# An expert stage that gathers for four experts at once, in one-pass products

## The chip, the cores and the metric

The kernel runs on one core of a Trainium2 chip. The metric is the device time of one execution in microseconds (us), the median of several runs. A core has a matrix engine (TensorE, PE in the profile; its weight loads stand apart as PEld), a vector engine (VectorE, DVE), a scalar engine (ScalarE, ACT), GpSimd (POOL), and SyncE (SP), which here issues all large transfers. Transfers are carried out by 16 DMA engines. TensorE writes its results into PSUM, from where DVE or ACT copy them out to SBUF, the working memory.

## What is computed

Two transformer blocks on 256 tokens of width 1024, in float32. The change touches only the last part of the second block, a mixture of experts:

```python
def hier_moe(h, w_group, b_group, w_expert, b_expert, w_gate, w_up, w_down):
    t = h.reshape(-1, d); hf = t.astype(F32)
    ...                                   # router: one of 4 groups, then the two best of its 8 experts
    combine = jnp.sum(jax.nn.one_hot(global_i, N_EXPERTS, dtype=F32) * top_w[..., None], axis=1)
    out = jnp.zeros(hf.shape, F32)
    for e in range(N_EXPERTS):            # 32 experts, w_gate and w_up 1024 x 512, w_down 512 x 1024
        hid = jax.nn.silu(t @ w_gate[e]) * (t @ w_up[e])
        out = out + combine[:, e:e + 1] * (hid @ w_down[e]).astype(F32)
    return out.reshape(bsz, seq, d).astype(h.dtype)
```

Each token takes part in two experts only; for all others its `combine` is zero.

## The kernel before

The kernel is written against a tile framework: the code allocates named tiles from pools, and a scheduler of the framework puts the instructions of every engine into a fixed order when the kernel is built, by priorities and its own idea of durations. Block 1 and the rest of block 2 come first; the change does not touch their code. At their end stands the stage of the experts (`moe`, L1323), in these steps:

- **Router.** For each half of the tokens (t = 0, 1) the normed row is made in two steps: L1352 multiplies x by the norm's weights on DVE, L1373 multiplies by the reciprocal root on ACT. The two tiles `hh` stay for the whole stage. A chain of some fifty small DVE instructions (L1371 to L1417) finds the two experts of each token, their weights (`comb`), and `rank`, the place of a token in its expert's list. Each expert takes up to 64 tokens (`CAP`); a token count above 64 would run a second path behind `tc.If` (L1534 on), and every engine reads the flag `oi` for it, SP among them (TENSOR_LOAD in the order of its instructions).
- **Loop over 16 pairs of experts** (L1514). For a pair p, `prepare` (L1430) builds a one-hot matrix `oh` on DVE from `rank`, and the same times the router's weight, `ow`. TensorE multiplies the token rows by `oh`, which gathers the 2 x 64 tokens as the columns of `xg`: 8 slices of the width (k) times two halves of the tokens. `hk` (L1428) picks a slice as every 8th element of a row of `hh`. `ow` is transposed to `owT`. `hidden` (L1467) makes the gate and up products (PSUM tiles `proj`) and the gated units (tile `th`). `down` (L1481) transposes these to `hT`, multiplies by the down weights (PSUM tiles `sc`) and copies the result out into `yo`. `scatter` (L1499) multiplies by `owT`, which weights the rows and puts them back to their tokens (PSUM tiles `pv` and `tp`), and adds to x.
- The code of the loop is hidden(p), scatter(p-1), prepare(p+1), down(p).

**Products and passes.** All products go through `mm` (L145). One on float32 operands stands as two MATMUL records in the trace, one on float32r operands as one; a transpose is one. Gate, up and down keep 64 columns of weights for each of two experts in two halves of the array, and their records run side by side in twos. Gather and put-back use all 128 columns.

**Weights.** The weights of the experts are read once, in 384 loads of 512 KB: for a pair 16 for gate and up (i = 0 to 3, two experts each) and 8 for down. `fetch` (L1454) takes a buffer for each from a ring of 36 (`RING`, L42: names w, h, l, x, u, T, t, which are the buffers wraw, whi, wlo, wx, u, Thi, Tlo of the earlier blocks). A load waits on SP until its buffer is free, and every load behind it on SP waits too. The u buffers are 16 and serve rows, gathered tokens and results as well.

Of the kernel before, what the change touches and what calls it, by code (L numbers as in the profile page):

```python
# [25 lines left out]
F32 = mybir.dt.float32  # L26
F32R = mybir.dt.float32r
AF = mybir.ActivationFunctionType
OP = mybir.AluOpType
# [9 lines left out]
HPR = 600  # L39

CAP = 64
RING = "w" * 5 + "h" * 5 + "l" * 4 + "x" * 5 + "u" * 9 + "T" * 4 + "t" * 4  # L42

SH1, SH2 = 0, 4
NEG = -1e30
# [74 lines left out]
def tile_model(ctx: ExitStack, tc: tile.TileContext, I: dict, out: bass.AP):  # L120
    nc = tc.nc
    V, S, G, T = nc.vector, nc.scalar, nc.gpsimd, nc.tensor
# [3 lines left out]
    psum = ctx.enter_context(tc.tile_pool(name="psum", bufs=1, space=PS))  # L126
# [8 lines left out]
    def wtile(shape, dt, name, bufs=2):  # L135
        return (scope[0] if name in common else scope[-1]).tile(shape, dt, name=name, bufs=bufs)
# [22 lines left out]
    ident_r = const.tile([128, 128], F32R, name="ident_r")  # L159
# [1144 lines left out]
    def runit(claim=False):  # L1304
        return unit(claim, F32R)
# [17 lines left out]
    def moe(router, wb, ring):  # L1323
# [20 lines left out]
        with tc.high_priority(HPR):  # L1344

            for c in range(2):
                for t in range(2):
                    cs = slice(512 * c, 512 * c + 512)
                    tsplit(x[:, t, cs], t, pair[c])
                    sq = wtile([128, 512], F32, name="th")  # L1350
                    S.activation(sq, x[:, t, cs], AF.Square, accum_out=ss[:, t, c:c + 1])
                    V.tensor_mul(hh[t][:, cs], x[:, t, cs], wb[:, cs])  # L1352
            ps = psum.tile([128, 512], F32, name="proj", bufs=3)
            for K in range(8):
                xh, xl = pair[K // 4]
# [9 lines left out]
            rs = rstd_of(r1, 2, 1024)  # L1365
            tp = psum.tile([128, 4, 128], F32, name="tp", bufs=2)
# [33 lines left out]
            comb = R_(32, "comb")  # L1400
# [12 lines left out]
            rank, many = R_(32, "rank"), R_(32, "many")  # L1413
# [11 lines left out]
            V.tensor_add(oh0, oh0, oh1)  # L1425
            spread(comb, oh0)

        hk = [h.rearrange("q (p k) -> q k p", k=8) for h in hh]  # L1428

        def prepare(p):  # L1430

            oh = wtile([128, 2, 2, CAP], F32, name="oh", bufs=2)
            ow = wtile([128, 2, 2, CAP], F32, name="ow", bufs=2)
            for t in range(2):
                full = [128, 2, CAP]
                V.tensor_tensor(oh[:, t], cnt_row[:, None, :].to_broadcast(full),  # L1436
                                rank[:, t, 2 * p:2 * p + 2, None].to_broadcast(full), op=OP.is_equal)
                V.tensor_tensor(ow[:, t], oh[:, t], comb[:, t, 2 * p:2 * p + 2, None].to_broadcast(full), op=OP.mult)
            ohv, owv = (o.rearrange("p t a s -> p t (a s)") for o in (oh, ow))
            xg = unit().rearrange("p (k s) -> p k s", k=8)  # L1440
            for k0 in (0, 4):
                tp = psum.tile([128, 4, 128], F32, name="tp", bufs=2)
                for k in range(4):
                    for t in range(2):
                        mm(tp[:, k, :], hk[t][:, k0 + k, :], ohv[:, t], t == 0, t == 1)
                (S.copy if k0 else V.tensor_copy)(xg[:, k0:k0 + 4, :], tp)
            tp = psum.tile([128, 4, 128], F32, name="tp", bufs=2)
            for t in range(2):
                T.transpose(tp[:, t, :], owv[:, t], ident)
            owT = wtile([128, 2, 128], F32, name="owT", bufs=2)  # L1450
            S.copy(owT, tp[:, 0:2])
            return xg, owT

        def fetch(nme, e, i):  # L1454
            with tc.high_priority(HPM):
# [8 lines left out]

        halves64 = (slice(0, CAP), slice(CAP, 2 * CAP))

        def hidden(p, xg):  # L1467
            pg, pu = (psum.tile([128, 512], F32, name="proj", bufs=3) for _ in range(2))
            for i in range(4):
                for ps, nme in ((pg, "w_gate_2"), (pu, "w_up_2")):  # L1470
                    ws = [fetch(nme, 2 * p + a, i) for a in range(2)]
                    for j in range(2):
                        k = 2 * i + j
                        for w, r in zip(ws, halves64):
                            mm(ps[r], xg[:, k, r], w[:, 512 * j:512 * j + 512], k == 0, k == 7)
            hid = wtile([128, 512], F32, name="th")
            S.activation(hid, pg, AF.Silu)  # L1477
            V.tensor_mul(hid, hid, pu)  # L1478
            return hid

        def down(p, hid):  # L1481
            tp = psum.tile([128, 4, 128], F32, name="tp", bufs=2)
            hv = hid.rearrange("s (p k) -> s k p", k=4)
            for k in range(4):
                T.transpose(tp[:, k, :], hv[:, k, :], ident)  # L1485
            hT = wtile([128, 4, 128], F32, name="hT", bufs=2)
            S.copy(hT, tp)  # L1487
# [6 lines left out]
            yo = unit().rearrange("p (c n) -> p c n", c=2)  # L1494
            S.copy(yo[:, 0], po[0])
            V.tensor_copy(yo[:, 1], po[1])  # L1496
            return yo

        def scatter(yo, owT):  # L1499
            for c in range(2):  # L1500
                cs = slice(512 * c, 512 * c + 512)
                for t in range(2):
                    ps = psum.tile([128, 512], F32, name="pv", bufs=1) if t == 0 else \
                        psum.tile([128, 4, 128], F32, name="tp", bufs=2).rearrange("p a s -> p (a s)")
                    mm(ps, owT[:, t], yo[:, c], True, True)
                    V.tensor_add(x[:, t, cs], x[:, t, cs], ps)

        def store():
            for c in range(2):
                for t in range(2):  # L1510
                    cs = slice(512 * c, 512 * c + 512)
                    nc.sync.dma_start(out[0, t * 128:(t + 1) * 128, cs], x[:, t, cs])

        ready, back = prepare(0), None  # L1514
        for p in range(16):
            xg, owT = ready
            hid = hidden(p, xg)
# [4 lines left out]
            back = down(p, hid), owT  # L1522
        scatter(*back)
        store()

# [9 lines left out]
        with tc.If(flag > 0):  # L1535
# [6 lines left out]
            for k in range(8):  # L1542
                tp = psum.tile([128, 4, 128], F32, name="tp", bufs=2)
                for t in range(2):
                    T.transpose(tp[:, t, :], hk[t][:, k, :], ident)
                V.tensor_copy(xa[k // 4][:, k % 4, :].rearrange("p (t s) -> p t s", t=2), tp[:, 0:2])
            with tc.For_i(0, 32) as e:
                V.tensor_scalar(turn, turn, 1.0, None, op0=OP.add)
# [4 lines left out]
                for t in range(2):  # L1553
                    ts = slice(128 * t, 128 * t + 128)
                    pg, pu = (psum.tile([128, 512], F32, name="proj", bufs=3) for _ in range(2))
                    for ps, nme in ((pg, "w_gate_2"), (pu, "w_up_2")):
                        for i in range(4):
                            w = ring()
                            nc.sync.dma_start(w.rearrange("p (j n) -> p j n", j=2),
                                              at(nme).rearrange("(p a j) n -> p a j n", a=4, j=2)[:, i])  # L1560
                            for j in range(2):
                                k = 2 * i + j
                                mm(ps, xa[k // 4][:, k % 4, ts], w[:, 512 * j:512 * j + 512], k == 0, k == 7)
                    hid = wtile([128, 512], F32, name="th")
# [3 lines left out]
                    tp = psum.tile([128, 4, 128], F32, name="tp", bufs=2)  # L1568
# [10 lines left out]
                    for c in range(2):  # L1579
                        cs = slice(512 * c, 512 * c + 512)  # L1580
# [3 lines left out]
    def run_moe(router, wb):  # L1584
# [12 lines left out]
        def ring():  # L1597
            turns[0] += 1
            return kinds[RING[(turns[0] - 1) % len(RING)]]()

# [39 lines left out]
```

## Time and profile before

| | us |
|---|---|
| median of 3 runs | 1891.49 (1889.62 to 1893.26) |
| the profiled execution, device time | 1893.15 |
| its span (first to last instruction) | 1891.3 |
| PE busy | 1780.4, 94% of the span |
| DVE, ACT, POOL busy | 1023.3, 704.0, 324.6 |
| DMA queue of the loads (q1) | 388.60 MB, 60.4% of 16 engines' span |

The page cuts the span into 40 slices of 47.3 us. The first 27 are blocks 1 and 2, with all engines at work. The last 13, from about 1290 us on, are the router and the experts: PE is at nine tenths throughout, DVE at one tenth, ACT and POOL near zero. The DMA engines, which run at three to six tenths in most slices before, stand between six and nine tenths here. A stage has its own limit, and the page's shares over the whole span don't tell which; so the trace is asked by stretches of this stage.

### The profile page before, as it was taken

The numbers are of one execution on the slowest core, as the hardware profiler recorded it, in microseconds if no ns is written. First come the engines' busy times: TensorE is split into PE (matmuls) and PEld (weight loads), VectorE is DVE, ScalarE is ACT, GpSimd is POOL, SyncE is SP. The second block draws the span as 40 slices with busy tenths as digits, with TensorE's granted clock in tenths as the row PEclk, the third lists the DMA queues.
The fourth block names the chain that finished last, engine by engine and source line by source line (L and its number), as shares of the span: only waits on it lengthen the run. The fifth ranks groups of instructions, "written<-read, shape, count | busy, mean of one in ns | idle before, by whom it ended". The sixth has DMA issues, their size and how long they took to land.

```text
span 1891.3 us, 24510 instructions
## 1 busy us (share of the span) xinstructions
PE 1780.4 (94%) x9197; PEld 1342.6 (71%) x9197; DVE 1023.3 (54%) x1662; ACT 704.0 (37%) x1343; POOL 324.6 (17%) x243
## 2 busy tenths in 40 slices
PE   7999999999999999999989888677999999999997
PEld 6999888888898998888777667556544444454542
DVE  7566657566745676756698997985111111111211
ACT  5455555554446565655465434132000000000000
POOL 1111134200121013210234434641000000000000
PEclk9999999999999999999999998888999999999999
DMA  8644445454566344536656321246799797979893
GB/s 253 186 134 140 148 143 154 144 181 151 166 184 183 111 129 145 159 105 200 202 146 176 92 90 45 89 150 256 311 357 408 288 411 284 412 291 406 342 359 120
DMA packets 186105, 390.19 MB, mean 206 GB/s; under 512 B 28608, under 2 KB 66688, under 8 KB 185984
## 3 DMA queue, kind: packets, MB, share of 16 engines
q1 hardware_dynamic: 185984, 388.60, 60.4%
q8 instruction: 73, 1.20, 0.3%
q14 instruction: 48, 0.39, 0.1%
HBM read 387.50 MB, written 1.05 MB: 205 GB/s over the span
## 4 chain that ended last, share of the span: by engine, by line
PE 83%; DVE 9%; issue 2%; POOL 2%; DMA 2%; ACT 2%; SPq 0%; ACTq 0%; DVEq 0%; POOLq 0%
PE proj L146 55%; PE sc L146 11%; PE tp L146 8%; PE pv L146 6%; DVE wlo L214 2%; PE tp L362 1%; PE tp L283 1%; DVE u L934 1%; DMA wraw<-in_w_in_dram 1%; PE tp L1485 1%; DMA u<-in_w_down_dram 1%; DMA whi<-in_w_down_dram 0%; ACT hT L1487 0%; DVE u L932 0%; POOL wlo L214 0%
## 5 line engine op out<-in xcount | busy, mean ns | idle before, releaser
L213 ACT CAST whi<-wraw 128x1024 fp32r<-128x1024 f32 x336 | 352.0, 1051 | 314.8 <-PE proj L146 262.6
L214 DVE TENSOR_TENSOR wlo<-wraw,whi 128x1024 fp32r<-128x1024 f32 (+1 forms) x285 | 371.6, 1307 | 169.0 <-PE proj L146 117.1
L146 PE MATMUL proj<-wlo,Thi 128*128 128x512 f32 (+1 forms) x1056 | 418.3, 396 | 5.6 <-DVE wlo L214 5.5
L146 PE MATMUL proj<-whi,Thi 128*128 128x512 f32 (+1 forms) x1056 | 417.8, 398 | 2.6 <-ACT P L985 1.0
L146 PE MATMUL proj<-whi,Tlo 128*128 128x512 f32 (+1 forms) x1056 | 414.9, 395 | 1.6 <-DVE Tlo L968 1.6
L146 PEld LDWEIGHTS proj<-wlo,Thi 128*128 128x128 f32 x1056 | 200.5, 190 | 47.6 <-DVE wlo L214 7.8
L146 PEld LDWEIGHTS proj<-whi,Thi 128*128 128x128 f32 x1056 | 200.6, 190 | 44.3 <-DVE u L1270 2.0
L146 PEld LDWEIGHTS proj<-whi,Tlo 128*128 128x128 f32 x1056 | 200.1, 189 | 42.4 <-DVE Tlo L968 2.1
L214 POOL TENSOR_TENSOR wlo<-wraw,whi 128x1024 fp32r<-128x1024 f32 (+1 forms) x51 | 131.2, 2572 | 428.5 <-PE proj L146 344.9
L146 PE MATMUL proj<-Thi,wlo 128*128 128x256 f32 x576 | 164.2, 287 | 4.4 <-DVE wlo L214 4.4
L146 PE MATMUL proj<-Thi,whi 128*128 128x256 f32 x576 | 163.2, 288 | 3.3 <-ACT Thi L955 2.3
L146 PE MATMUL proj<-Tlo,whi 128*128 128x256 f32 x576 | 163.0, 287 | 0.0
L146 PEld LDWEIGHTS tp<-oh,u 128*128 128x128 f32 x512 | 125.3, 335 | 13.6 <-issue 9.5
L146 PE MATMUL tp<-oh,u 128*128 128x128 f32 x512 | 125.5, 402 | 1.2 <-DVE oh L1436 1.2
L1478 DVE TENSOR_TENSOR th<-th,proj 128x512 f32<-128x512 f32 x16 | 11.0, 687 | 212.9 <-PE proj L146 199.4
L146 PEld LDWEIGHTS proj<-Thi,wlo 128*128 128x128 f32 x576 | 111.7, 194 | 4.8 <-DVE wlo L214 4.6
L146 PEld LDWEIGHTS proj<-Thi,whi 128*128 128x128 f32 x576 | 110.7, 194 | 5.2 <-ACT Thi L955 2.9
L146 PE MATMUL sc<-u 128*128 128x256 f32 (+1 forms) x416 | 99.8, 356 | 12.8 <-DVE u L927 12.8
L146 PEld LDWEIGHTS proj<-Tlo,whi 128*128 128x128 f32 x576 | 110.9, 194 | 0.2
L1496 DVE COPY u<-sc 128x512 f32<-128x512 f32 x16 | 11.1, 692 | 167.7 <-PE sc L146 167.7
L1477 ACT ACTIVATE th<-proj 128x512 f32<-128x512 f32 x16 | 9.6, 597 | 202.7 <-PE proj L146 202.6
L146 PEld LDWEIGHTS sc<-u 128*128 128x128 f32 x416 | 69.8, 196 | 20.7 <-issue 12.9
(452 smaller groups left out, 2481.3 us busy)
## 6 DMA issues: line engine op xcount, KB each, us to landing
wraw<-in_w_in_dram SPq DMA_DIRECT2D x236, 512.0 KB, 3.8
wraw<-in_w_proj_dram SPq DMA_DIRECT2D x48, 512.0 KB, 3.9
u<-in_w_up_dram SPq DMA_DIRECT2D x35, 512.0 KB, 10.2
u<-in_w_down_dram SPq DMA_DIRECT2D x30, 512.0 KB, 10.2
u<-in_w_gate_dram SPq DMA_DIRECT2D x30, 512.0 KB, 10.2
wraw<-in_w_gate_dram SPq DMA_DIRECT2D x28, 512.0 KB, 9.1
wx<-in_w_up_dram SPq DMA_DIRECT2D x27, 512.0 KB, 9.5
whi<-in_w_down_dram SPq DMA_DIRECT2D x25, 512.0 KB, 10.2
```

Of the source, the lines that this page charges most:

```text
L146: T.matmul(o, l, r, start=start, stop=stop)
L213: S.copy(hi[:, :, :n], raw[:, :, :n])
L214: (G if share[0] and scount[0] % share[0] == 0 else V).tensor_sub(lo[:, :, :n], raw[:, :, :n], hi[:, :, :n].bitcast(F32))
L283: T.transpose(ps[:, b, :], src[:, b * 128:(b + 1) * 128], ident)
L362: T.transpose(tp[:, j, :], P[:, j * 128:(j + 1) * 128], ident)
L934: V.tensor_tensor(v2(B), v2(m), st, op=OP.mult)
L1477: S.activation(hid, pg, AF.Silu)
L1478: V.tensor_mul(hid, hid, pu)
L1485: T.transpose(tp[:, k, :], hv[:, k, :], ident)
L1496: V.tensor_copy(yo[:, 1], po[1])
```

## The change

Five edits. The rows of the tokens are stored slice by slice, so that `hk` reads 128 elements that lie together. They are kept as two float32r parts, `hh` (rounded) and `hl` (the rest), and the gather multiplies both by a float32r one-hot of four experts (256 columns): 8 slices x 2 halves x 2 parts for a quad, in place of 8 slices x 2 halves for each pair. `ow` is gone: the one-hot itself is transposed (`ohT`), the router's weights are brought to the gathered order by two products with two columns per pair (`cg`), and one DVE instruction applies them together with the gate. The results of `down` are split into two float32r parts `yh` (ACT) and `yl` (DVE), and the put-back multiplies both by `ohT`. The ring has five u buffers in place of nine; rows and results take more of them than before.

```diff
-RING = "w" * 5 + "h" * 5 + "l" * 4 + "x" * 5 + "u" * 9 + "T" * 4 + "t" * 4
+RING = "w" * 5 + "h" * 5 + "l" * 4 + "x" * 5 + "u" * 5 + "T" * 4 + "t" * 4
...
-        hh = [unit(True), unit(True)]
+        hs, hh, hl = [unit(True), unit(True)], [runit(True), runit(True)], [runit(True), runit(True)]
+        hk, hlk = ([h.rearrange("q (k p) -> q k p", k=8) for h in hx] for hx in (hh, hl))
+        hp = [h.rearrange("q (k p) -> q p k", k=8) for h in hs]
...
-                    V.tensor_mul(hh[t][:, cs], x[:, t, cs], wb[:, cs])
+                    V.tensor_mul(hp[t][:, 64 * c:64 * c + 64, :], x[:, t, cs].rearrange("q (p k) -> q p k", k=8),
+                                 wb[:, cs].rearrange("q (p k) -> q p k", k=8))
...
-                S.mul(hh[t], hh[t], rs[:, t:t + 1])
+                S.mul(hh[t], hs[t], rs[:, t:t + 1])
+                V.scalar_tensor_tensor(hl[t], hs[t], rs[:, t:t + 1], hh[t].bitcast(F32), op0=OP.mult, op1=OP.subtract)
...
-        def prepare(p):
-            oh = wtile([128, 2, 2, CAP], F32, name="oh", bufs=2)
-            ow = wtile([128, 2, 2, CAP], F32, name="ow", bufs=2)
...
-                V.tensor_tensor(ow[:, t], oh[:, t], comb[:, t, 2 * p:2 * p + 2, None].to_broadcast(full), op=OP.mult)
...
+        def prepare(q):
+            oh = wtile([128, 2, 4, CAP], F32R, name="oh", bufs=1)
...
+                for k in range(2):
+                    for n, (src, t) in enumerate(((hk, 0), (hlk, 0), (hk, 1), (hlk, 1))):
+                        mm(tp[:, k, :], src[t][:, k0 + k, :], ohv[:, t], n == 0, n == 3)
...
+                for t in range(2):
+                    T.transpose(tp[:, t, :], rows[t], ident)
+                for t in range(2):
+                    mm(tp[:, 2, 0:2], rows[t], comb[:, t, 4 * q + 2 * a:4 * q + 2 * a + 2], t == 0, t == 1)
...
-            V.tensor_mul(hid, hid, pu)
+            V.scalar_tensor_tensor(hid, hid, cg, pu, op0=OP.mult, op1=OP.mult)
...
-            S.copy(yo[:, 0], po[0])
-            V.tensor_copy(yo[:, 1], po[1])
+            for c in range(2):
+                S.copy(yh[:, c], po[c])
+                V.tensor_sub(yl[:, c], po[c], yh[:, c].bitcast(F32))
...
-                    mm(ps, owT[:, t], yo[:, c], True, True)
+                    mm(ps, ohT[:, t], yh[:, c], True, False)
+                    mm(ps, ohT[:, t], yl[:, c], False, True)
...
-            if p < 15:
-                ready = prepare(p + 1)
+            if not ready and p < 15:
+                ready = prepare(p // 2 + 1)
```

The order of the instructions of blocks 1 and 2 is the same in both programs up to the router. Three places where it differs follow; in a row of the order stand line, operation, output and inputs, the output's size and a count.

On TensorE, where one pair is put back and the next tokens are gathered, the program before has this (`pv` and `tp` are PSUM tiles, u holds rows, results or weights):

```order
L146 MATMUL sc<-Tlo,hT 64x512 x8
L146 MATMUL pv<-u,owT 128x512
L146 MATMUL tp<-u,owT 128x512 x2
L146 MATMUL pv<-u,owT 128x512
L146 MATMUL tp<-oh,u 128x128 x16
L1449 MATMUL tp<-ident,ow 128x128 x2
L1485 MATMUL tp<-ident,th 128x128 x4
```

and the changed program this, for a quad:

```order
L146 MATMUL pv<-u,ohT 128x512
L146 MATMUL tp<-u,ohT 128x512
L146 MATMUL pv<-u,ohT 128x512
L146 MATMUL tp<-u,ohT 128x512 x3
L146 MATMUL pv<-u,ohT 128x512 x2
L146 MATMUL tp<-oh,u 128x256 x32
L1455 MATMUL tp<-ident,oh 128x128 x2
L146 MATMUL tp<-comb,oh 128x2 x2
L1455 MATMUL tp<-ident,oh 128x128 x2
L146 MATMUL tp<-comb,oh 128x2 x2
```

Sixteen gathering products per pair became 32 of twice the columns per quad, four products of the put-back became eight, and four small ones with two columns came in per quad.

On SP, at the start of the stage, the program before reads the flag and then issues loads of the second round of the ring; the first loads into u buffers (down weights of the first pair) stand behind 16 others:

```order
L1461 DMA Thi<-in_w_up_dram 128x1024
L1534 TENSOR_LOAD oi
L1534 ISA x2
L1461 DMA wraw<-in_w_gate_dram 128x1024 x2
L1461 DMA wraw<-in_w_up_dram 128x1024 x2
L1459 DMA wraw<-in_w_down_dram 128x1024
L1459 DMA whi<-in_w_down_dram 128x1024 x5
L1459 DMA wlo<-in_w_down_dram 128x1024 x2
L1461 DMA wlo<-in_w_gate_dram 128x1024 x2
L1461 DMA wx<-in_w_up_dram 128x1024 x2
L1459 DMA u<-in_w_down_dram 128x1024 x5
```

In the changed program they stand right behind the flag:

```order
L1473 DMA Thi<-in_w_up_dram 128x1024
L1549 TENSOR_LOAD oi
L1549 ISA x2
L1471 DMA u<-in_w_down_dram 128x1024 x5
L1473 DMA wraw<-in_w_gate_dram 128x1024 x2
L1473 DMA wraw<-in_w_up_dram 128x1024 x2
```

Ahead of the flag both have the same 27 loads of expert weights; 357 follow.

On DVE, in the router, the two new instructions that make `hl` (L1378) stand ahead of the router's logits:

```order
 L289 TENSOR_SCALAR rstd<-r1s 128x2
 L285 SCALAR_TENSOR_TENSOR Tlo<-tp,Thi 128x4x128 x2
-L1371 SCALAR_TENSOR_TENSOR lg<-tp,rstd_11951,wrb 128x36 x2
-L1297 TENSOR_REDUCE r_11961<-lg 128x2
-L1298 TENSOR_TENSOR ohg<-lg,r_11961 128x8
...
+L1378 SCALAR_TENSOR_TENSOR u<-u,rstd_11959 128x1024 x2
+L1375 SCALAR_TENSOR_TENSOR lg<-tp,rstd_11959,wrb 128x36 x2
+L1297 TENSOR_REDUCE r_11971<-lg 128x2
```

The logits (`lg`), and all of the chain behind them, now come after these two.

## Rows read from the trace of the kernel before

**Rows 1.** The page's 40 slices: PE busy in tenths; GB/s moved.

```profile
PE   7999999999999999999989888677999999999997
...
GB/s 253 186 134 140 148 143 154 144 181 151 166 184 183 111 129 145 159 105 200 202 146 176 92 90 45 89 150 256 311 357 408 288 411 284 412 291 406 342 359 120
```

**Rows 2.** Stretches: length, busy us (records) of PE, PEld, DVE, ACT, POOL; PEclk, DMA share, GB/s.

```profile
1400.00:1460.00 60.00, 57.40 (x243) 30.87 (x243) 11.31 (x22) 4.67 (x9) 0.00 (x0) 1.00 1.03 411
1500.00:1550.00 50.00, 48.58 (x213) 21.69 (x210) 6.57 (x13) 3.81 (x7) 0.00 (x0) 1.00 1.03 413
...
1800.00:1850.00 50.00, 48.58 (x210) 21.57 (x208) 4.82 (x7) 3.60 (x7) 0.00 (x0) 1.00 1.00 388
...
1315.00:1885.00 570.00, 550.10 (x2272) 274.80 (x2272) 90.94 (x178) 43.55 (x81) 0.00 (x0) 1.00 0.85 332
```

**Rows 3.** The chain that ended last, around one pair: start us, us, what.

```profile
1506.61 1.06 PE pv L146 x2
1507.66 1.72 PE tp L146 x4
1509.38 0.86 PE pv L146 x2
1510.24 7.53 PE tp L146 x32
...
1517.98 12.18 PE proj L146 x56
```

**Rows 4.** Groups by line and shape, 1290 to 1895 us: busy us, mean ns.

```profile
L146 PE MATMUL tp<-oh,u 128*128 128x128 f32 x512 | 125.5, 402 | 1.2 <-DVE oh L1436 1.2
L146 PEld LDWEIGHTS tp<-oh,u 128*128 128x128 f32 x512 | 125.3, 335 | 13.6 <-issue 9.5 <-DVE u L1446 2.4
...
L1495 ACT COPY u<-sc 128x512 f32<-128x512 f32 x16 | 9.4, 586 | 112.0 <-PE sc L146 104.4 <-DMA wx<-in_w_gate_dram 7.6
```

**Rows 5.** Chain pieces of float32r products in block 1: 256 columns, then 512.

```profile
99.84 11.21 PE proj L146 x93
...
849.45 6.62 PE proj L146 x29
```

**Rows 6.** SP's loads, the flag and the transfers around the stage's start.

```profile
1309.91 0.33 SPq L1461 DMA_DIRECT2D Thi<-in_w_up_dram  x1
...
1325.21 0.81 SPq L1461 DMA_DIRECT2D wraw<-in_w_gate_dram  x2
...
1316.46 0.15 DVE L1533 CAST oi<-om 128x1 int32<-128x1 f32 x1
...
1315.00:1320.00 5.00, 4.79 (x20) 4.82 (x21) 1.83 (x11) 0.00 (x0) 0.00 (x0) 0.62 0.66 262
1320.00:1325.00 5.00, 5.00 (x23) 3.71 (x25) 1.36 (x5) 0.86 (x2) 0.00 (x0) 1.00 0.00 0
1325.00:1330.00 5.00, 5.00 (x26) 1.72 (x24) 0.00 (x0) 0.00 (x0) 0.00 (x0) 1.00 0.76 236
```

**Rows 7.** Issues of loads by kind: count, KB each, us to landing.

```profile
u<-in_w_up_dram SPq DMA_DIRECT2D x35, 512.0 KB, 10.2
```

**Rows 8.** DVE: multiply-and-subtract over 1024 columns; the router's first logits.

```profile
L299 DVE SCALAR_TENSOR_TENSOR u<-x,rstd,rowb x4: 1277/1283/1284, 6.8 to 482.7; 128x1024 f32<-128x1024 f32 x4
...
1307.22 0.42 DVE L1371 SCALAR_TENSOR_TENSOR lg<-tp,rstd,wrb 128x36 f32<-128x36 f32 x2 [2.66 <-PE tp L146]
```

**Rows 9.** The end of the chain that ended last: the last pair's way out.

```profile
1871.74 0.49 PE tp L1485 x4
...
1880.13 0.57 ACT u L1495
...
1884.48 0.69 DVE x L1506
```

**Rows 10.** Two stretches in which TensorE waits: clock granted (third from the end).

```profile
1310.00:1315.00 5.00, 0.63 (x2) 0.50 (x2) 4.54 (x35) 0.00 (x0) 0.00 (x0) 0.50 1.03 407
1345.00:1350.00 5.00, 3.87 (x18) 1.62 (x17) 0.90 (x4) 1.45 (x3) 0.00 (x0) 1.00 1.03 419
```

More of the change, by code (lines that the diff above doesn't have):

```diff
@@ L1426, in moe @@
             spread(comb, oh0)
-        hk = [h.rearrange("q (p k) -> q k p", k=8) for h in hh]
-        def prepare(p):
-            oh = wtile([128, 2, 2, CAP], F32, name="oh", bufs=2)
-            ow = wtile([128, 2, 2, CAP], F32, name="ow", bufs=2)
+        def prepare(q):
+            oh = wtile([128, 2, 4, CAP], F32R, name="oh", bufs=1)
             for t in range(2):
-                full = [128, 2, CAP]
+                full = [128, 4, CAP]
                 V.tensor_tensor(oh[:, t], cnt_row[:, None, :].to_broadcast(full),
-                                rank[:, t, 2 * p:2 * p + 2, None].to_broadcast(full), op=OP.is_equal)
-                V.tensor_tensor(ow[:, t], oh[:, t], comb[:, t, 2 * p:2 * p + 2, None].to_broadcast(full), op=OP.mult)
-            ohv, owv = (o.rearrange("p t a s -> p t (a s)") for o in (oh, ow))
-            xg = unit().rearrange("p (k s) -> p k s", k=8)
-            for k0 in (0, 4):
-                tp = psum.tile([128, 4, 128], F32, name="tp", bufs=2)
[L1443 to L1452, printed above, removed]
@@ new lines, in prepare @@
+                                rank[:, t, 4 * q:4 * q + 4, None].to_broadcast(full), op=OP.is_equal)
+            ohv = oh.rearrange("p t a s -> p t (a s)")
+            xg = []
+            for k0 in range(0, 8, 2):
+                if k0 % 4 == 0:
+                    xg.append(unit().rearrange("p (k s) -> p k s", k=4))
+                tp = psum.tile([128, 4, 128], F32, name="tp", bufs=2).rearrange("p (k a) s -> p k (a s)", k=2)
+                for k in range(2):
+                    for n, (src, t) in enumerate(((hk, 0), (hlk, 0), (hk, 1), (hlk, 1))):
+                        mm(tp[:, k, :], src[t][:, k0 + k, :], ohv[:, t], n == 0, n == 3)
+                (S.copy if k0 % 4 else V.tensor_copy)(xg[-1][:, k0 % 4:k0 % 4 + 2, :], tp)
@@ new lines, in prepare @@
+            got = []
+            for a in range(2):
+                rows = [ohv[:, t, 128 * a:128 * a + 128].bitcast(F32) for t in range(2)]
+                tp = psum.tile([128, 4, 128], F32, name="tp", bufs=2)
+                for t in range(2):
+                    T.transpose(tp[:, t, :], rows[t], ident)
+                for t in range(2):
+                    mm(tp[:, 2, 0:2], rows[t], comb[:, t, 4 * q + 2 * a:4 * q + 2 * a + 2], t == 0, t == 1)
+                ohT = wtile([128, 2, 128], F32R, name="ohT", bufs=4)
+                S.copy(ohT, tp[:, 0:2])
+                cg = wtile([128, 1], F32, name="cg", bufs=4)
+                for j in range(2):
+                    V.tensor_copy(cg[64 * j:64 * j + 64], tp[64 * j:64 * j + 64, 2, j:j + 1])
+                got.append(([(xg[k // 4], k % 4) for k in range(8)], 128 * a, cg, ohT))
@@ L1454, in fetch @@
+            return got
         def fetch(nme, e, i):
@@ L1474, in hidden @@
                         for w, r in zip(ws, halves64):
-                            mm(ps[r], xg[:, k, r], w[:, 512 * j:512 * j + 512], k == 0, k == 7)
+                            xk = xg[k][0][:, xg[k][1], a + r.start:a + r.stop]
+                            mm(ps[r], xk, w[:, 512 * j:512 * j + 512], k == 0, k == 7)
             hid = wtile([128, 512], F32, name="th")
             S.activation(hid, pg, AF.Silu)
-            V.tensor_mul(hid, hid, pu)
+            V.scalar_tensor_tensor(hid, hid, cg, pu, op0=OP.mult, op1=OP.mult)
             return hid
@@ L1493, in down, with scatter @@
                         mm(po[c][r], hT[:, k, r], w[:, 512 * c:512 * c + 512], k == 0, k == 3)
-            yo = unit().rearrange("p (c n) -> p c n", c=2)
-            S.copy(yo[:, 0], po[0])
-            V.tensor_copy(yo[:, 1], po[1])
-            return yo
-        def scatter(yo, owT):
+            yh, yl = (runit().rearrange("p (c n) -> p c n", c=2) for _ in range(2))
+            for c in range(2):
+                S.copy(yh[:, c], po[c])
+                V.tensor_sub(yl[:, c], po[c], yh[:, c].bitcast(F32))
+            return yh, yl
+        def scatter(yh, yl, ohT):
             for c in range(2):
@@ L1515, in moe @@
         for p in range(16):
-            xg, owT = ready
-            hid = hidden(p, xg)
+            xg, a, cg, ohT = ready.pop(0)
+            hid = hidden(p, xg, a, cg)
             if back is not None:
                 scatter(*back)
-            if p < 15:
-                ready = prepare(p + 1)
-            back = down(p, hid), owT
+            if not ready and p < 15:
+                ready = prepare(p // 2 + 1)
+            back = *down(p, hid), ohT
         scatter(*back)
@@ L1544, in moe @@
                 for t in range(2):
-                    T.transpose(tp[:, t, :], hk[t][:, k, :], ident)
+                    mm(tp[:, t, :], hk[t][:, k, :], ident_r, True, False)
+                    mm(tp[:, t, :], hlk[t][:, k, :], ident_r, False, True)
                 V.tensor_copy(xa[k // 4][:, k % 4, :].rearrange("p (t s) -> p t s", t=2), tp[:, 0:2])
```

2 lines of the change are left out of this document (1 added, 1 removed).

## The prediction

> **What bounds the kernel now.** I read the page's slices first [rows 1], then the last stage by stretches [rows 2], then the chain that ended last [rows 3], and only then single groups. The slices show that the stage of the experts has PE at nine tenths from end to end, while the rate of transfers swings between about 285 and 412 GB/s. That swing is the thing to see: a queue that limits doesn't swing. In its best stretches it moves 411 and 413 GB/s for 50 and 60 us with a DMA share of 1.03, so this is what the queue can do when it is let; over the stage it averages 332, because loads wait for buffers that TensorE hasn't finished with. From 1315 to 1885 us PE is busy 550 of 570 us at a clock of 1.00, that is its 2.4 GHz level [rows 2]. So TensorE bounds the stage, with some 20 us of waits, and the chain consists of its products [rows 3]. DVE, with 91 of 570 us, and ACT with 44 have ample room. The queue has little: it is second, not idle.
>
> **The time against which I sum.** The profiled execution took 1893.15 us, 1.7 above the median of 1891.49; its span is 1891.3, so 1.9 us lie around the span. The sum is made on the span and 1.9 added. The order of blocks 1 and 2 is unchanged, so everything up to the router stays.
>
> **The change on TensorE, part by part.**
>
> *Gather.* A pair's gather is 32 records in 7.53 us [rows 3], 0.235 us each; 16 pairs make 120.5 us (the 512 records of the group are busy 125.5 [rows 4]). After it there are 8 quads of 32 float32r records with 256 columns. Block 1 does just this, with 128 columns of weights that lie together: 93 such records in 11.21 us, 0.1205 each [rows 5]. So 8 x 32 x 0.1205 = 30.8 us: the gather gives back 89.7. The first gather of the stage may run at the lower clock, as the stretch from 1315 does (0.62 [rows 6]); I take off 1.7 us for it. That leaves 88. If the cadence stayed at 0.235 (a rival, below), the gain would be 60 instead of 90.
>
> *Put-back.* A pair's four products take 1.06 + 1.72 + 0.86 = 3.64 us as eight float32 records [rows 3]. As eight float32r records of 512 columns, at 6.62 / 29 = 0.228 each [rows 5], they take 1.83. But the low part needs one more step: ACT's copy (0.59 [rows 4]), then DVE's subtraction, and the additions into x queue on DVE behind both subtractions, at about 0.69 each (the last addition of the stage [rows 9]). Placing these by hand, the last product starts when the first addition has freed its PSUM tile, some 2.6 us after the first product. Gain between 0.9 and 1.8 us for a pair; I take 1.0, near the end that the DVE steps set: 16 us.
>
> *Router's weights.* Four small products per quad are 32 products, 64 records. The trace has no product of two columns; the nearest rows are transposes, 4 in 0.49 us [rows 9], 0.12 each. 64 x 0.11 = 7 us added; with no cost at all it would be 0. The two transposes per pair remain, and of the one-hot products on DVE half go.
>
> *DVE and ACT.* In a pair DVE gets two subtractions and loses a copy and two small products, about 0.7 us more on an engine that is busy 91 of 570. The cover is TensorE's 7 us of down products; if DVE had none, it would be 16 x 0.7 = 11 us. The strided write of the normed rows has no row of its own; I take the 0 that equal sizes suggest, at most 1 us.
>
> *Router.* The two new DVE instructions (1.28 us each [rows 8]) stand ahead of the logits, which start at 1307.22 [rows 8]. The first can start when ACT has made the first `hh`, about 1305.1, the second ends near 1307.65. So the chain behind moves by 0.45 us, at most by 2.6 if they started late.
>
> *TensorE's end.* 88 + 16 - 7 - 0.5 = 96.5 us less: the last addition would come at 1885.2 - 96.5 = 1788.7, the span's end 6.1 us later as before, at 1794.8, the time 1797. That keeps all 20 us of waits; without them it is 1777. So TensorE could be done between 1777 and 1797.
>
> **What is late next: the queue.** In the changed order, as before, 27 loads stand ahead of the flag and 357 behind it. A load is 512 KB [rows 7], 524,288 bytes; at 411 GB/s [rows 2] it takes 1.276 us, and 357 take 455.4. When can this stream start? Before, nothing is issued between 1309.91 and 1325.21, and the queue runs dry: 262 GB/s in 1315 to 1320, which is full rate until about 1318, then 0 [rows 6]. SP can't pass the flag before DVE has cast it (1316.46 + 0.15 [rows 6], 0.45 later now); reading it I put at 1 us. Five loads of the first pair's down weights then follow at once, where before the next load waited for TensorE. Bytes follow an issue by some 1.9 us: 236 GB/s over the stretch from 1325 means full rate from 1327.1 after an issue at 1325.21 [rows 6]. So the stream starts at about 1320. While these five land, TensorE frees the first buffers. From there a pair costs the queue 24 x 1.276 = 30.6 us and TensorE some 28 to 29 (570 / 16 = 35.6, less 6), so TensorE is the quicker of the two and the queue doesn't stop for buffers. The last load lands at 1320 + 455.4 = 1775.4.
>
> The last loads issued are up weights of the last pair. Behind them come four products in halves (1.7 us), the unit's multiplication (0.9 with its wait), and all that lies from the transposes at 1871.74 to the end of the span at 1891.3 [rows 9], 19.6 us, less 0.8 in the put-back: 21.4. End of the span 1796.8, time 1798.7. Against the median I state **1798 us**, ratio 0.95.
>
> **A rule weighed.** The row shows 411 to 413 GB/s held for 50 and 60 us [rows 2]. The Trainium skill (DMA: Bandwidth & Descriptors, Specifications) gives a core about 358 GB/s as its share of the HBM, under a ceiling of 435 for the path into SBUF. By the row the 357 loads take 455 us; by the page's 358 they would take 523 (an estimate from that page), and the time would be 1866. The trace does not agree with the lower figure in stretches of this length; no run here yet shows 450 us on end.
>
> **The rivals.**
>
> 1. *The queue sets the end*, as above: 1798. For it: the two ends are within 2 us even with all of TensorE's waits kept, and these waits partly go. With 402 to 419 GB/s (the spread of five-us stretches, 419 in [rows 10]) the last load lands 9 us earlier or 10 later: 1789 to 1809.
> 2. *TensorE still sets the end.* The queue is quicker than I think, or starts sooner, and the waits in TensorE's order remain: 1797 at most by the sum, 1785 with half the waits. For it: the two ends nearly meet. Its times lie within the same range.
> 3. *The gather stays bound by loading weights.* Its weight loads last 335 ns in the trace [rows 4]; were it not the step of eight elements but their number that sets 0.235 us, the 256 records would cost 29.4 us more, and TensorE's end would be 1797 + 29 = 1826. Against: block 1's 0.1205 with equal sizes [rows 5].
> 4. *The rate sags when the queue has no pauses.* The stretch from 1800 shows 388 [rows 2]: at that, 357 loads take 482 us, 27 more: 1825. Against: that stretch contains waits of its own. The rule above is the sharper form of this rival.
> 5. *Slower than before, by the clock.* TensorE now waits for loads in every pair. From 1310 to 1315 it works 0.63 of 5 us and the clock stands at 0.50, its 1.2 GHz level [rows 10]. The gate, up and down products of a pair are 96 records; 12.18 us for 56 [rows 3] makes 20.9 us a pair, 334 in all, and as much again at the lower level. Half of them at that level costs 167 us: 1797 + 167 = 1964. It turns the sign from 95 us on, that is from 28% of these products. Against: between 1345 and 1350 TensorE waits 1.1 of 5 us for loads and keeps 1.00 [rows 10], and the wait I expect is about 2 us in 30, in several pieces.
>
> That the change doesn't do what it says is excluded: the order shows the 256-column products and the pairs of parts.
>
> **How the numbers follow.** Chances: queue 0.66, TensorE 0.16, gather 0.07, sagging rate 0.08, clock 0.03. The range takes in 1 and 2 with their bounds (1789 to 1809, and 1787 if the flag is read sooner), and reaches to the two cases at 1825: **1787 to 1826**. A measurement here tells 0.2% from no change: faster by more than that 0.96, within it 0.01, slower 0.03.
>
> **What would show it.** In the profile after: records of the gather about 0.12 us apart, the put-back's about 0.23 where they don't wait; a steady 405 to 415 GB/s in every stretch from 1330 to 1770 in place of the swing; waits of TensorE on loads in every pair; a chain with DMA pieces in its later part; about 21 us from the last landing to the end. Wrong would be a swing that stays (then TensorE or the order of loads bounds), a clock under 1.00 in the stage, or a gather near 7 us per quad.

## The result, and the profile after

The changed kernel takes 1818.68 us (median of 4, 1817.13 to 1821.45) against 1892.34 beside it: a ratio of 0.961 (0.960 to 0.963), 74 us gained. The forecast was 1798: the sign and most of the size are right, some 20 us are missing. The profiled execution has a span of 1816.9 us, where the sum came to 1796.8.

The page's slices (the rows that answer to [rows 1], with the granted clock) show that the swing in the rate is gone:

```profile
PE   7999999999999999999998988867799999999997
...
PEclk9999999999999999999999999988899999999999
...
GB/s 251 194 133 149 135 152 123 139 197 166 142 185 202 134 138 118 122 174 111 233 165 170 154 93 94 47 93 144 277 382 379 409 409 407 409 408 409 407 380 154
```

From 1385 to 1745 us the queue moves 406 to 410 GB/s in every stretch of 30 us, as forecast. It falls short at the start, around 1370 and from 1745 on. Stretches of the stage (columns as in [rows 2]):

```profile
1320.00:1325.00 5.00, 5.00 (x22) 1.77 (x20) 0.69 (x1) 0.00 (x0) 0.00 (x0) 0.87 0.90 287
...
1370.00:1375.00 5.00, 4.53 (x22) 1.64 (x24) 0.18 (x2) 0.42 (x1) 0.00 (x0) 1.00 0.64 200
...
1600.00:1640.00 40.00, 36.80 (x168) 16.15 (x166) 11.06 (x21) 4.82 (x9) 0.00 (x0) 1.00 1.03 409
...
1745.00:1750.00 5.00, 5.00 (x18) 1.50 (x16) 0.00 (x0) 0.00 (x0) 0.00 (x0) 0.70 0.81 295
1765.00:1780.00 15.00, 14.97 (x72) 5.12 (x68) 0.75 (x1) 0.60 (x1) 0.00 (x0) 1.00 0.99 374
1785.00:1790.00 5.00, 4.91 (x21) 1.87 (x18) 2.22 (x4) 1.17 (x2) 0.00 (x0) 1.00 0.29 118
```

Two pieces of the chain at the same place of the program, four pairs apart, give the pace of the middle:

```profile
1495.96 1.96 PE sc L146 x8
...
1618.95 1.96 PE sc L146 x8
```

122.99 us for 96 loads are 1.281 us a load, and 524,288 bytes at 409 GB/s take 1.282. So here the queue sets the pace, and TensorE waits: for loads, and, in pieces of 0.7 to 0.9 us, for ScalarE and VectorE (what TensorE waited for from 1320 to 1815 us: us in total, times, longest):

```profile
PE sc L146 <- ACT hT L1500: 8.5, 12, 0.7
PE proj L146 <- DMA wraw<-in_w_gate_dram: 5.8, 4, 1.9
PE proj L146 <- DMA wlo<-in_w_gate_dram: 5.5, 6, 1.9
```

With the smaller ones the loads make 14.5 us. But the end belongs to TensorE. The last load, by the 118 GB/s of its stretch, lands at 1786.4; the chain before it is this, with the last transfer that TensorE waits for in front:

```profile
1753.54 10.04 DMA u<-in_w_gate_dram
...
1763.62 15.67 PE proj L146 x72
...
1780.70 7.09 PE sc L146 x32
...
1790.56 5.31 PE proj L146 x22
...
1798.23 8.81 PE sc L146 x32
...
1810.11 0.65 DVE x L1521
```

From 1763.6 on TensorE has work with no pause over 0.9 us, and the queue waits for slots (buffers of the ring) that TensorE must free: between 1763 and 1780 SP waits 8.3 us for gate and up products. Of the signs that the prediction named, the waits for loads in every pair did not come: they stand at seven places from 1423 us on, up to 1.9 us long.

### The profile page after: what moved, and what is told of

Read it like the earlier page. It is cut to its first block, busy times and chain, and to the rows that moved or that the text cites. A ratio compares the mean times of both kernels' runs of the same rounds, so it can differ in the third digit from the quotient of the medians.

```text
span 1816.9 us, 24162 instructions
## 1 busy us (share of the span) xinstructions
PE 1696.3 (93%) x9005; PEld 1262.6 (69%) x9005; DVE 1029.8 (57%) x1664; ACT 714.2 (39%) x1359; POOL 324.9 (18%) x247
## 4 chain that ended last, share of the span: by engine, by line
PE 74%; DVE 10%; DMA 10%; issue 2%; POOL 2%; ACT 1%; SPq 0%; DVEq 0%; ACTq 0%; POOLq 0%
PE proj L146 54%; PE sc L146 10%; PE pv L146 5%; DMA u<-in_w_gate_dram 3%; DMA wraw<-in_w_gate_dram 2%; PE tp L146 2%; DVE wlo L214 2%; PE tp L362 1%; PE tp L283 1%; DMA whi<-in_w_gate_dram 1%; DVE u L934 1%; DMA wraw<-in_w_in_dram 1%; DMA wlo<-in_w_up_dram 1%; DMA wlo<-in_w_down_dram 1%; DMA Tlo<-in_w_gate_dram 1%
## 5 line engine op out<-in xcount | busy, mean ns | idle before, releaser
L1510 DVE TENSOR_TENSOR u<-sc,u 128x512 fp32r<-128x512 f32 x32 | 22.1, 691 | 190.5 <-ACT u L1509 190.2
L1491 DVE SCALAR_TENSOR_TENSOR th<-th,cg,proj 128x512 f32<-128x512 f32 x16 | 12.0, 748 | 162.1 <-PE proj L146 102.0
L353 ACT ACTIVATE P<-sc,nm 128x256 f32<-128x256 f32 (+1 forms) x152 | 63.7, 432 | 33.2 <-DVE nm L346 20.2
L1509 ACT CAST u<-sc 128x512 fp32r<-128x512 f32 x32 | 18.7, 586 | 101.5 <-PE sc L146 91.4
```

The source lines that it names most:

```text
L353: S.activation(P[:, i * nS:(i + 1) * nS], scv[:, i, :], AF.Exp, bias=nm[:, i:i + 1], accum_out=l_out[:, i:i + 1])
L1491: V.scalar_tensor_tensor(hid, hid, cg, pu, op0=OP.mult, op1=OP.mult)
L1509: S.copy(yh[:, c], po[c])
L1510: V.tensor_sub(yl[:, c], po[c], yh[:, c].bitcast(F32))
```

## The experiments

The runs are called e1 to e12 here; the number stands ahead of each expectation. e2, e3, e4 and e6 were executed once, the others four or five times; e2, e3 and e6 leave out bytes or products, as said there.

**The order of the loads, each side alone, and the layout.** The loads on SP's queue don't stand in the order in which TensorE uses them; the first theory laid the 20 us to that. The edit puts them in the written order:

```diff
-  nc.sync.dma_start(w, src...)
+  tc.keep_in_program_order(nc.sync.dma_start(w, src...))
```

*e1*, expected:

> The changed kernel (1818.7 us) with one difference: the 384 loads of the experts' weights stand on SP's queue in the order in which the code names them, which is the order in which TensorE uses them; so far a load stood up to 20 places behind its turn and up to 30 ahead of it. Ring, bytes and arithmetic are the same. Theory A, that the 20 us missing against the forecast come from the order of the loads (the queue waits for slots of tiles that TensorE reaches late, and TensorE waits for loads that stand late): the queue keeps 405 to 412 GB/s to its last load, that lands near 1775 us, and the time is 1795 to 1803 us. Theory B, that TensorE's own work is longer than summed: no change, 1815 to 1821 us. Theory C, that the queue cannot hold 411 GB/s over the whole stage whatever waits for it: 1811 to 1818 us, the last landing still near 1786 us.

1825.07 us, 6 us slower than the change, which no theory had. The queue moves 409 GB/s from 1340 to 1785 us, as theory A had it, but TensorE is no longer held by loads: it waits for none, and instead (1320 to 1815 us):

```profile
PE tp L1498 <- DVE th L1491: 13.0, 14, 0.9
PE sc L146 <- ACT hT L1500: 10.1, 14, 0.7
PE pv L146 <- ACT u L1509: 9.2, 14, 0.7
```

Those are 32.3 us. With loads in order the framework's scheduler also lays TensorE's products in the written order (gate and up, then down of the same pair), and each pair stands still behind silu, the copy of the transposed units and the copy of y. The irregular order had filled most of these with the next pair's products, and so needed its loads early. On the same chain the clock falls four times behind such a stop, which shows in a pair's down products; once with the fall, once without:

```profile
1459.88 8.88 PE sc L146 x32
...
1496.35 7.18 PE sc L146 x32
```

Four falls of 1.7 us each are 6.8, on top of the waits.

Then loads of half the bytes, `w[:, 0:512]` read for every product:

*e2*, expected:

> The changed kernel with each expert load cut to half of its bytes (256 KB), every product still made, from the half that was loaded, so that the products use the wrong half of the weights: what TensorE takes when the queue cannot hold it up. Theory A: TensorE alone would be done by 1780 to 1795 us, time 1785 to 1800 us, and it waits for no load after 1330 us. Theory B, TensorE's own work is longer than summed: 1812 to 1820 us, as with whole loads.

1816.59 us: by the number theory B, but not by its mechanism. The queue's share falls to 0.5 to 0.8, and still TensorE waits for loads of u tiles (8.0 us in 3 waits), and the window from 1360 to 1440 has the clock at 0.96:

```profile
PE proj L146 <- DMA u<-in_w_up_dram: 8.0, 3, 3.1
```

These loads were issued late, not carried slowly. The scheduler had also laid out the orders of TensorE and of the loads anew for the shorter loads, with pieces of gather and put-back between the gate and up products, so this run is no clean measure of TensorE alone; a later one is.

Then half the products, whole loads:

*e3*, expected:

> The changed kernel with all loads whole, but only half of the products of the expert layers made (one of the two row blocks of each gate and up tile, one of the two column halves of each down tile): TensorE has 18 us of work in a pair where the queue has 30.6. What the queue takes when TensorE frees every slot early. Theory A: 405 to 412 GB/s from 1320 us to the last landing near 1772 us, time 1785 to 1793 us. Theory C, the queue cannot hold 411 GB/s over the stage: last landing near 1786 us, time 1798 to 1806 us.

1805.69 us. The rate isn't the reason: it is 409 or 410 GB/s from 1360 to 1760 us. But even with TensorE busy for only 288 of these 400 us SP stops for slots, and the last load lands near 1784:

```profile
1760.00:1765.00 5.00, 4.63 (x16) 1.15 (x18) 0.00 (x0) 0.00 (x0) 0.00 (x0) 1.00 0.54 207
1765.00:1770.00 5.00, 5.00 (x26) 1.90 (x24) 0.75 (x1) 0.60 (x1) 0.00 (x0) 1.00 0.92 268
```

So even a TensorE with half the products ends 8 us behind the forecast. The scheduler had laid the loads in another order than the changed kernel's here too, so what the changed kernel's own order costs isn't measured by this run. And the layout, `hk` read as before with a step of eight:

```diff
-  hk, hlk = ([h.rearrange("q (k p) -> q k p", k=8) for h in hx] for hx in (hh, hl))
+  hk, hlk = ([h.rearrange("q (p k) -> q k p", k=8) for h in hx] for hx in (hh, hl))
```

*e4*, expected:

> The changed kernel with the normed tokens left in their old order (channel 8p+k), so that the gather's 128x128 weights are read with a stride of 8 elements again; hi and lo parts, four experts at once and everything else as in the change. If the layout sets the records' spacing (the rival put at 0.07 in the prediction), a quad's gather goes from 3.9 us to 7.5 us or more, which is 29 us of TensorE over 8 quads; TensorE waits some 10 us for loads in four pairs, so some of it is hidden: 1825 to 1850 us. If the layout does not matter, 3.9 us and 1816 to 1821 us.

1830.12 us. A quad's gather, in the changed kernel and here (timelines of TensorE: start us, us, what):

```profile
1415.67 4.16 PE L146 MATMUL tp<-oh,u 128*128 128x256 f32 x32
```

```profile
1365.15 8.01 PE L146 MATMUL tp<-oh,u 128*128 128x256 f32 x32
```

Contiguous tokens halve it: 0.25 us a record with the step, 0.13 without. The first quad, which begins at the lower clock, gains less. All eight, in the changed kernel and then with the step (1300 to 1890 us; busy us, mean ns):

```profile
L146 PE MATMUL tp<-oh,u 128*128 128x256 f32 x256 | 36.4, 300 | 1.3 <-DVE oh L1438 1.3
```

```profile
L146 PE MATMUL tp<-oh,u 128*128 128x256 f32 x256 | 64.6, 412 | 1.4 <-DVE oh L1436 1.4
```

These are 28.2 us more of work, and the time grew by 11.4; the order of the loads is the same in both. TensorE's waits for loads fell from 14.5 to 4.1 us, which takes up 10.4, and its gate and up products (all records of the tile `proj`, 1312 to 1890 us) from 256.3 to 250.5 us, which takes up 5.9 and nearly closes the sum. A microsecond of TensorE is worth some 0.4 here.

**The order of both written out.** The down products of a pair go behind the gate and up products of the next, and both queues keep the written order:

```diff
+  kp = tc.keep_in_program_order      # around every product, transpose and load of the loop
 for p in range(16):
     hid = hidden(p, xg, a, cg)
+    if held is not None:
+        hT = turn_hidden(held[0])      # transposes and copy of pair p-1
     if back is not None:
         scatter(*back)
     if not ready and p < 15:
         ready = prepare(p // 2 + 1)
-    back = *down(p, hid), ohT
+    if held is not None:
+        back = *down(p - 1, hT), held[1]
+    held = hid, ohT
```

*e5*, expected:

> The changed kernel with the order of TensorE and of the loads written out: the down products of a pair come after the gate and up products of the next pair, so that silu, the copy of the transposed units and the copies of y lie beside other products; TensorE and the loads keep the written order, so loads stand in the order of use; in the ring the u tiles come last. Arithmetic and bytes are the same. Theory D (after the runs before: the 20 us are lost by order, as loads that stand late and TensorE's short waits for ScalarE and VectorE, each about 0.7 to 0.9 us, some two in a pair; the work of neither TensorE nor the queue is longer than its sum by more than 5 us): TensorE has 26 to 28 us of work a pair, the queue 24 x 1.282 = 30.8 us and sets the pace, the last load lands near 1780 us, 14 us follow, time 1793 to 1799 us. Theory B (TensorE's own work is longer than summed): 1812 us or more.

1803.37 us (ratio 0.952, 0.951 to 0.954), 15 us under the change. The queue is at 408 to 410 GB/s in every stretch from 1310 to 1780 us, and the longest of TensorE's waits for a load is 0.9 us:

```profile
1560.00:1600.00 40.00, 38.19 (x170) 15.94 (x168) 7.47 (x15) 4.27 (x8) 0.00 (x0) 1.00 1.03 409
...
1780.00:1785.00 5.00, 4.52 (x22) 2.26 (x20) 3.39 (x6) 1.76 (x3) 0.00 (x0) 1.00 1.01 404
1785.00:1790.00 5.00, 5.00 (x26) 1.83 (x24) 0.47 (x1) 0.00 (x0) 0.00 (x0) 1.00 0.43 170
```

The expectation missed by 4 us, since the last load lands at 1787, not 1780: the pinned loads start later (see e9). Three things changed at once here, the order of the loads, the later down products and the place of the u tiles in the ring; what each gives alone was not run, but for the loads (e1). The same order with half loads is the clean measure:

*e6*, expected:

> The kernel of the run before with each expert load cut to half of its bytes, every product still made (with the wrong half of the weights), and TensorE's instructions in exactly the same order: what TensorE alone takes. Theory D: 26 to 28 us a pair, done by 1745 to 1775 us, time 1755 to 1785 us. Theory B: 1805 us or more.

1753.48 us, 1.5 under the range of theory D. Theory B is out: the same products in a good order take TensorE this long, chain of two pairs:

```profile
1441.03 13.73 PE proj L1436 x64
...
1457.48 4.52 PE tp L1436 x34
...
1463.44 7.02 PE sc L1436 x32
1470.46 13.73 PE proj L1436 x64
...
1487.39 7.02 PE sc L1436 x32
1494.40 6.00 PE proj L1436 x27
```

From 1441.03 to 1494.40 are 53.4 us, 26.7 a pair, where the queue needs 30.8. Two more: the flag's load behind the last expert load (`with tc.issue_after(last_load): flag = nc.values_load(...)`) and the changed kernel with its put-back in one f32 product again:

*e7*, expected:

> The kernel with the written order, and the load of the overflow flag behind the last expert load on SP's queue instead of behind the 27th, where SP stands still for it for some 6 us and the queue fell to 287 to 294 GB/s for 10 us. If the queue sets the end, these 3 us are gained whole: 3 us under the run with the flag in its old place, 1790 to 1796 us. If TensorE sets it: no difference to that run.

1802.56 us (0.951 to 0.953 of before): not told apart from the 1803.37, and not the 3 us expected of a queue that sets the end. In the pinned kernel the loads come so late that SP reaches the flag when it is there; 1310 to 1320 is at 408 with the flag in its old place.

```diff
-  mm(ps, ohT[:, t], yh[:, c], True, False)
-  mm(ps, ohT[:, t], yl[:, c], False, True)
+  mm(ps, ohT[:, t], yo[:, c], True, True)
```

*e8*, expected:

> The changed kernel with the put-back in two parts undone: y stays one f32 tile and is put back in one f32 product, with the one-hot in f32 (the router's weight stays on the gated units). The prediction gave the split 1.0 us a pair, 16 us of TensorE in all, of which the forecast (queue sets the end) sees almost nothing at the end. If the queue sets the pace over most of the stage, TensorE's waits for loads, 8 us in four pairs, hide the longer put-back: 1816 to 1824 us. If TensorE sets it: 1832 to 1848 us.

1820.98 us, 0.961 of before like the change itself. In the changed kernel the put-back's two parts are worth nothing that can be measured, though its records (the readers of `ohT`, 1312 to 1890 us) take TensorE 60.8 us here and 43.4 there. TensorE's waits for loads fell from 14.5 to 10.0 us and its gate and up products from 256.3 to 251.5; what covers the rest isn't placed.

**The start of the stream, and the put-back where TensorE bounds.** The loads of SP ahead of the stage, in the changed kernel:

```profile
1254.82 0.81 SPq L1473 DMA_DIRECT2D wx<-in_w_up_dram  x2
1255.68 1.66 SPq L1471 DMA_DIRECT2D wx<-in_w_down_dram  x3
```

Pinned, the same tiles wait for their turn behind others:

```profile
1305.28 1.25 SPq L1478 DMA_DIRECT2D wx<-in_w_up_dram  x2
1306.58 1.79 SPq L1478 DMA_DIRECT2D wx<-in_w_gate_dram  x2
```

So the ring begins with them, and the first 27 loads aren't pinned:

```diff
-RING = "w" * 5 + "h" * 5 + "l" * 4 + "x" * 5 + "u" * 5 + "T" * 4 + "t" * 4
+RING = "x" * 5 + "w" * 5 + "h" * 5 + "l" * 4 + "T" * 4 + "t" * 4 + "u" * 5
```

*e9*, expected:

> The kernel with the written order and the flag behind the last load, with one difference: the ring begins with the five wx tiles, whose memory is free some 50 us before the others, and the first 27 loads may go out as soon as their slots are free, as in the changed kernel. With all loads pinned the queue moved 10.9 MB from 1250 to 1310 us, in the changed kernel 14.5 MB, which is 7 loads or 9 us at 409 GB/s. If the queue sets the end over the whole stage, the last load lands 6 to 9 us earlier, near 1779 us, and the time is 1793 to 1797 us. If TensorE sets it: 1800 to 1803 us, no difference.

1795.89 us (1794.96 to 1797.37), ratio 0.9485 (0.947 to 0.950): the best version, 23 us under the change. The last load lands near 1779, as expected. In every 40 us from 1360 to 1760 the rate is 409 or 410 and the clock 1.00:

```profile
1560.00:1600.00 40.00, 37.90 (x173) 16.16 (x174) 7.47 (x15) 4.27 (x8) 0.00 (x0) 1.00 1.03 409
...
1775.00:1780.00 5.00, 4.57 (x20) 1.88 (x22) 2.17 (x4) 0.00 (x0) 0.00 (x0) 1.00 0.80 321
```

*e10*, expected:

> The same kernel with the flag's load in its old place behind the 27th expert load. With the first loads early SP stands still for the flag again while the queue runs empty, 2.5 to 3 us at some 290 of 409 GB/s for 10 us in the changed kernel: 2 to 4 us slower than the run before if the queue sets the end; no difference if TensorE does.

1797.04 us against 1795.89, with intervals that overlap (0.947 to 0.951, and 0.947 to 0.950): the 2 to 4 us of the expectation can't be told from nothing; by the slowest run here and the fastest there the flag's place costs under 3 us. Without the flag's stop the queue falls as low a little later (280 and 249 GB/s in 1320 to 1330), now for slots.

*e11*, expected:

> The kernel before (1893 us), where TensorE sets the pace, with the put-back in two parts and the router's weight on the gated units, and the gather as it was; the ring has two u tiles fewer for y's second part. By the prediction's terms: 16 us gained by the put-back (bounds 14 to 29) and 7 us lost by the two-column products: 1871 to 1886 us, most likely 1884. If TensorE's waits for y's two parts take back what the products gain: 1890 us or more.

1877.56 us, 0.9915 of before (0.9897 to 0.9934): a gain of 12 to 20 us, 16.9 by the medians, where the terms gave 9. Where TensorE bounds, the put-back does pay; the same part is worth nothing in the changed kernel (e8). The put-back's own records, in the kernel before and here (columns as in [rows 2], the instructions that read `owT` or `ohT`):

```profile
1312.00:1890.00 578.00, 59.21 (x128) 23.00 (x128) 6.03 (x16) 0.99 0.84 331
```

```profile
1312.00:1890.00 578.00, 42.86 (x128) 20.34 (x128) 5.96 (x16) 0.98 0.84 329
```

That is 16.3 us, where 16 were summed, and the two-column products take 8.1, where 7 were. So the gain beyond the 9 does not lie in these two terms. TensorE's waits from 1320 us on fell from 19.2 to 15.9 us and its gate and up products by some 3; the order of the loads and the ring differ as well, and the rest isn't placed.

**Only the last pair's loads in order.** The edit of the first experiment, for the last 24 loads alone.

*e12*, expected:

> The changed kernel (1818.7 us) with the loads of the last pair alone in the order of use: its eight down loads go behind its last five gate and up loads, which so far were issued last (1774.6 to 1778.3 us) and landed by about 1786 us, with silu, the down products and the put-back still to come; TensorE's order and everything before are unchanged. If the 9 us by which the changed kernel's end lies further behind the last landing than in the forecast come from what was loaded last: the five land by about 1778 us and the time is 1807 to 1813 us. If the five were late because their slots came free late, the loads behind them are late as well, and the time is 1816 to 1821 us: no gain.

1819.04 us, no gain. The number is that of the second branch, its reason isn't: the five loads were issued at 1764.0 to 1768 instead of 1774.6 to 1778.3, and the end stayed. Now the down loads land last, near 1787, and the chain behind the transfer is the old one, 1.4 us later at its start:

```profile
1754.82 10.18 DMA u<-in_w_gate_dram
...
1765.05 15.67 PE proj L146 x72
...
1799.67 7.18 PE sc L146 x32
```

So at the end the changed kernel lacks no load; TensorE has 46 us of work left at 1764, its short waits included. That it is so late there comes from the hold-ups before, which is inferred and not run.

## Why the prediction was right, and what it lost 20 us on

*TensorE's terms.* The gather was right: 4.0 to 4.2 us a quad instead of 15.1 for two pairs (some 6 for the first, at the lower clock), and e4 confirms that the step of eight was the reason (the rival at 0.07 would have been the 8.0 us seen there). The put-back's size per pair was right in the changed kernel, 2.8 us from 1787.79 to 1790.56 against 3.64 [rows 3], waits included, and so was its gain in e11, 16.3 us of records for 16; the router's weights cost 8.1 for 7. "TensorE some 28 to 29" us a pair was high: 26.7 in e6, whose order has fewer waits. The flag's reading, put at 1 us without a row, took 1.1 in the changed kernel, from the end of the cast at 1315.63 to the next load at 1316.69.

*The queue's price.* 411 GB/s from stretches of 50 and 60 us [rows 2] became 409, held for 400 us in e9: 1.282 instead of 1.276 us a load, and 357 x 0.006 = 2.1 us. The rival of a sagging rate is out, and with it the rule weighed: the rows show 409, not the 358 GB/s of the Trainium skill (DMA: Bandwidth & Descriptors, Specifications). The same page says (Bandwidth, Measured) that the share is what a core gets while the other core of its pair streams too; this program runs on one core, and the trace agrees with that reading; no run here has the other core streaming.

*The step that failed* is the sentence "TensorE is the quicker of the two and the queue doesn't stop for buffers". TensorE's work is shorter than the queue's, but its order and that of the loads tie the two together: a load waits for the slot of a tile that TensorE reaches late, TensorE waits for a load that stands behind. SP at the second stop, in the changed kernel, and what it waits for there:

```profile
1363.62 0.33 SPq L1471 DMA_DIRECT2D whi<-in_w_down_dram  x1
1372.43 0.81 SPq L1473 DMA_DIRECT2D whi<-in_w_gate_dram  x2
```

```profile
SPq L1473 <- PE sc L146: 7.6, 1, 7.6
```

The bill for the last landing, forecast at 1775.4 and found at 1786.4, against a stream of 409 from 1320 on (for each stretch its length times the missing share of 409): rate 2.1; start, 1320 to 1340, 1.8; stop at 1370 to 1385, 3.4; stops from 1745 to 1760 and from 1765 to 1780, 4.0. Together 11.3, for 11.0.

The tail, forecast at 21.4, is 30.5: at the last landing TensorE still has 4.1 us of the pair before (to 1790.5); behind it stand 22 records of gate and up, 5.3 us instead of 1.7 for eight; and the last 32 down records take 8.81 instead of 7.1, at a clock of 0.74 from 1800 to 1805. Together 9.4, for 9.1.

*The rivals.* Neither of the first two alone: the queue sets the pace for most of the stage, TensorE the last 50 us. That the forecast's 1798 could be had with the same arithmetic is shown by e9, at 1796, where the step holds from 1340 us on. The clock fell, as the last rival had it, but for some 3.5 us each at 1423, 1744 and 1799, not for half of the products; at the last fall that cost 1.7 us (8.81 for 7.1). That the measured time lies inside the stated range owes something to luck: the range reaches to 1826 for two other cases, a gather bound by its weights and a sagging rate, and neither came. The weak point was in sight: the order of loads and the ring of 32 were there to read, and the two ends were within 2 us of each other, and here two resources that wait for one another lost to both sums.

## What to carry to other kernels

When two resources come out within a few per cent of each other, don't take the later of the two ends: look whether the order in which one asks is the order in which the other delivers, and price what each holds up. An order of use isn't enough by itself: with the loads in the written order, and TensorE's products laid in it too, the kernel was 6 us slower (e1), since every pair then waited for silu and the copies. With the down products one pair later both orders together gave 15 us (e5), and 23 with the first loads early (e9). What a part of a change is worth depends on what bounds while it is there: the put-back and the router's weights gave 17 us in one kernel, and undoing the put-back cost nothing that can be measured in the other.

## What was not expected of the hardware

The granted clock fell to 0.50, its 1.2 GHz level, after quite small gaps: it stands there from 1424 to 1427, from 1745 to 1747.5 and from 1799.5 to 1802.5. Eight gate records at 1423 take 4.53 us, 0.57 each instead of 0.22 (partly waits):

```profile
1423.12 4.53 PE L146 MATMUL proj<-wraw,u 128*64 128x512 f32 x8 [1.84 <-DMA wraw<-in_w_gate_dram]
```

Before the falls at 1423 and 1744 TensorE did gather, transposes and two-column products, before that at 1800 transposes, each with waits of 0.7 to 1.9 us; a wait of 1.9 us at 1508 between gate products left the clock at 1.00. In e1 the same place of a pair, with the same waits, fell four times and held the other times. What decides isn't settled. In e9, where such work stands between long products with waits of at most 0.5 us, the granted clock is 1.00 over the whole of 1360 to 1785.
